# Swiglus in halves of 11 gate tiles instead of thirds, weight-block sums written over their blocks, and the last swiglu with all high parts before all low parts

## The chip, the cores and the metric

The kernel runs on one core of a Trainium2 chip. The metric is the device time of one execution in microseconds (us), and the time of a kernel is the median of its runs. Engines are named as in the profile: PE (TensorE matmul), PEld (its weight load), DVE (VectorE), ACT (ScalarE), POOL (GpSimd) and SP (SyncE, which here issues nearly all DMA).

## The reference

A two-layer diffusion transformer on 256 latent and 256 context tokens, width 1024, in float32. Each layer is swiglu, mixer, swiglu; layer 0 mixes with a short convolution, layer 1 with attention. Every step is modulated by vectors that come from matrix-vector products with `mod_w`.

```python
def _modulate(t, g, shift, scale):
    return _rms(t, g) * (1 + scale) + shift

def _swiglu(h, w13, w2):
    gte, up = jnp.split(h @ w13, 2, axis=-1)
    return (jax.nn.silu(gte) * up) @ w2
...
    for i in range(DEPTH):
...
        mod = (jax.nn.silu(c) @ mod_w[i] + mod_b[i]).reshape(bsz, 3, 3, 1, D_MODEL)
        modc = (jax.nn.silu(c_ctx) @ mod_w[i] + mod_b[i]).reshape(3, 3, D_MODEL)
        lat = lat + 0.5 * mod[:, 0, 2] * _swiglu(_modulate(lat, norm_g[i, 0], mod[:, 0, 0], mod[:, 0, 1]), ffn_w13[i, 0], ffn_w2[i, 0])
...
        lat = lat + mod[:, 1, 2] * y
...
        lat = lat + 0.5 * mod[:, 2, 2] * _swiglu(_modulate(lat, norm_g[i, 2], mod[:, 2, 0], mod[:, 2, 1]), ffn_w13[i, 1], ffn_w2[i, 1])
    return lat
```

The hidden width is 2816, which is 22 gate tiles of 128. The context tokens go through the first swiglu of layer 0, the convolution, the second swiglu of layer 0 and the first swiglu of layer 1; the last swiglu of layer 1 works on the 256 latent tokens alone.

## The kernel before

**Precision.** A float32 product is made of three fast matmuls: each operand is split into a high part (ACT copies it to the reduced format, L107) and a low part (DVE subtracts, L108), and `mm3` (L127) adds high×high, high×low and low×high in PSUM. So every weight costs ACT one pass and DVE one pass before PE may use it. Halves of split weights are tiles `wh`/`wl` of 1024 columns (4 of each, L110).

**Stages.** Opening; swiglu `ffn(0, 0)`; convolution mixer; its output product (`cw_out`); `ffn(0, 1)`; `ffn(1, 0)`; attention; the last swiglu. The residual `x` lies with features on partitions and 512 tokens (256 latent, 256 context) on columns.

**`ffn` (L632)** goes through the 22 gate tiles in three parts of 8, 7 and 7 (`THIRDS`). In each part it first makes the part's gate tiles g and then calls `project` (L483), which multiplies them with the part's rows of w2 for the 8 output tiles m and adds the result to `x` (L467: two instructions of 256 columns for each m and part). A raw tile of w2 holds two m's; each m is split in one piece of 1024 or 896 columns.

**`Pair` (L554)** computes one gate tile's two products (gate and up, 512 tokens each) with seven half-size products instead of eight. In a pair, `head` uses the blocks A11 and A12 of the weight, `five` the sum S1, `six` S2 and S4, `seven` S3, `four` A22; 84 matmuls of 256 columns in all. PE runs them as `head`, `five`, the previous pair's `seven`, `six`, the previous pair's `four`. `sums` (L572) makes S1 to S4 from the raw weight `wr` with three DVE instructions (L578 1024 columns; L584 and L588 512 columns) into a tile `ws` of its own, of which there is one; then ACT and DVE split `ws`. Three raw tiles `wr` are shared by all weight and modulation loads (`load_raw`, L101), which SP issues one after the other. The DVE ends of a pair are `sg` (L618, waits for `six`), `gm` (L629, waits for `four`) and the sum p (L623, waits for `seven`). All but 12 of the 66 gate tiles of these three swiglus go this way, 54 pairs; the others go as plain products (`w13_mm`, L540).

**Modulation.** 224 units (L151, one DVE instruction over 128x1024 each, four or two to a raw tile of 1 MB) make the modulation vectors. `tick(n)` (L190) issues n of them at fixed places in the program: `ev` after each output tile of a projection, 0.5 in each pair, 3 in a plain gate tile, 6 in each step of the convolution.

**Order.** A list scheduler sets the order of instructions on each engine from the program's order and its own estimates; every engine then runs its own list in order. Only the opening, parts of the attention and the start of the last swiglu are written out by hand.

**End of a projection.** Where a projection ends a stage, the last two m's are done in token halves so that the norm of the latent half starts early (`late`, L526). `square_add` (L231) sums the squares for the norm on DVE, 256 columns at a time.

**Last swiglu (L1567 on).** Activations hold high and low part side by side in 512 columns. `mm2` (L1432) issues for each block the high weight against 512 columns, then the low weight against the 256 high columns.

Of the kernel before, what the change touches and what calls it, by code (L numbers as in the profile page):

```python
# [16 lines left out]
P = 128  # L17
# [5 lines left out]
THIRDS = (8, 7, 7)  # L23

AS_IS = {(0, 0): range(3, 8), (0, 1): (), (1, 0): ()}
# [15 lines left out]
def hybrid_kernel(ctx: ExitStack, tc: tile.TileContext, a: dict, out: bass.AP):  # L41
# [5 lines left out]
    gp = ctx.enter_context(tc.tile_pool(name="gp", bufs=8))  # L47
# [47 lines left out]
    sccol = const.tile([P, KT, 32], F32, name="sccol", tag="sccol")  # L95
# [135 lines left out]
    def square_add(k, c0, c1):  # L231

        n = c1 - c0
        sq = tp.tile([P, T2], F32, name=nm("sq"), tag="gm", bufs=3)
        nc.scalar.activation(out=sq[:, :n], in_=x[:, k, c0:c1], func=AF.Square)
        for s in range(2):
            if c0 <= s * S < c1:
                part = sq[:, s * S - c0 : s * S - c0 + S]
                if k == 0:
                    accs[s] = tp.tile([P, S], F32, name=nm("acc"), tag=f"acc{s}", bufs=1)  # L240
                    nc.vector.tensor_copy(accs[s], part)
                elif k < KT - 1:
                    nc.vector.tensor_tensor(out=accs[s], in0=accs[s], in1=part, op=ALU.add)
                else:
                    accs[s, "last"] = part
# [237 lines left out]
    def project(ws, src, nk, gate, tail, tot, late, ev, between=()):  # L483
# [10 lines left out]
        nf = 3 if between else 2  # L494
        ahead = {}

        def get(m):
            for i in range(m, min(m + 3, KT)):
                if i not in ahead:
                    ahead[i] = ws(i)  # L500
            return ahead[m]

        w2 = [get(m) for m in range(nf)]
        p2 = [psum("py") for _ in range(nf)]
        cut = nk - 2 if between else nk - 1
        for i in range(nf):
            products(p2[i], w2[i], range(cut), 0, tot)
            if i < len(between):
                between[i]()
        if between:  # L510
            for i in range(nf):
                products(p2[i], w2[i], (nk - 2,), 0, tot)
        for i in range(nf):
# [4 lines left out]
        for m in range(nf, KT - late):  # L518
# [6 lines left out]
            tick(ev)  # L525
# [27 lines left out]

    class Pair:  # L554
# [11 lines left out]
        def keep(self, keys, part):  # L566
            hi, lo = half()
            split(hi, lo, part)
# [3 lines left out]
        def sums(self, n):  # L572

            a21, a22, a11, a12 = (self.raw[:, i * T2 : i * T2 + T2] for i in range(4))
            tt = nc.vector.tensor_tensor
            if n == 0:
                self.sm = sm = wp.tile([P, 2048], F32, name=nm("ws"), tag="ws", bufs=1)
                tt(  # L578
                    out=sm.rearrange("p (a b c) -> p a b c", a=2, b=2)[:, :, 0, :],
                    in0=a21.unsqueeze(1).to_broadcast([P, 2, T2]),  # L580
                    in1=self.raw[:, T2 : 3 * T2].rearrange("p (a c) -> p a c", a=2),
                    op=ALU.subtract,
                )
                tt(out=sm[:, T2:1024], in0=a11, in1=sm[:, :T2], op=ALU.subtract)  # L584
                self.keep(("S1", "S2"), sm[:, :1024])
                return
            sm = self.sm
            tt(out=sm[:, 3 * T2 :], in0=a12, in1=sm[:, T2:1024], op=ALU.subtract)  # L588
            self.keep(("S3", "S4"), sm[:, 1024:])
            self.w["A22"] = [  # L590
                wp.tile([P, T2], F32R, name=nm(t), tag=t, bufs=2) for t in ("w4h", "w4l")
            ]
            split(*self.w["A22"], a22)
# [38 lines left out]
    def ffn(l, b, h, tot, gate, tail, gs=(), ev=1.5):  # L632
        gs = list(gs)
        i0 = 0
        for t, n in enumerate(THIRDS):
            between = ()
            if tot == T2:
# [22 lines left out]
                for i in range(len(gs), n):  # L660
                    if t == 0 and not heads and i in AS_IS[l, b]:
# [15 lines left out]
                        else:  # L677
                            tick(3)
# [31 lines left out]
            box = {}  # L710

            def ws2(m):
                if m // 2 not in box:
                    src = a["w2a"][l, b, m // 2] if t == 0 else a["w2b"][l, b, t - 1, m // 2]
                    box[m // 2] = load_raw(src, 2 * n * P)
# [1011 lines left out]
```

## Time and profile before

| | |
|---|---|
| median of 3 runs | 1584.11 us (1583.46 to 1584.88) |
| the profiled execution's own time | 1585.98 us |
| its span, first to last instruction | 1584.1 us |
| mean granted TensorE clock | 0.991 |
| PE busy | 1562.8 us (99%) |
| DVE busy | 1318.2 us (83%) |
| ACT busy | 731.5 us (46%) |
| DMA | 248.74 MB, mean 157 GB/s |

PE's stages lie as follows (us of the span): opening to 55, `ffn(0, 0)` 55 to 378, convolution 378 to 519, `cw_out` 519 to 565, `ffn(0, 1)` 565 to 913, `ffn(1, 0)` 914 to 1270, attention 1271 to 1392, last swiglu 1392 to 1580. Matmuls are pipelined: what one costs PE is the distance between two starts, not the duration shown. The granted clock is 1.00 at full speed; a stretch of half speed costs half its length.

### The profile page before, as it was taken

How to read it: one execution, taken by the hardware profiler on the slowest of the kernel's cores; microseconds unless marked ns; L12 is line 12 of the kernel's file. 1: busy time of each engine (PE TensorE's matmuls, PEld its weight loads, DVE VectorE, ACT ScalarE, POOL GpSimd, SP SyncE). 2: the span in 40 equal slices, each digit the busy share in tenths (PEclk: the TensorE clock that was granted, in tenths of full speed). 3: DMA queues.
4: the chain of work that ended last, by engine and by line, in shares of the span. 5: the costliest groups of instructions: out<-in, count | busy, mean ns of one | idle time of the engine just before them, and what ended most of it. 6: DMA issues, size and time to landing. Idle time of an engine off the chain costs nothing.

```text
span 1584.1 us, 24975 instructions
## 1 busy us (share of the span) xinstructions
PE 1562.8 (99%) x10192; PEld 1425.7 (90%) x10192; DVE 1318.2 (83%) x2001; ACT 731.5 (46%) x1165; POOL 34.2 (2%) x28
## 2 busy tenths in 40 slices
PE   9999999999999999999999999999999989999998
PEld 7788998999878899989899899899889889998887
DVE  5788889879998879889799899898898886788654
ACT  4522552535222366335346375345245255765543
POOL 0000000000000000000000000000000002320000
PEclk8999999999999999999999999999999989999999
DMA  9355234334465422532443423543543652257552
GB/s 347 149 208 211 81 124 159 130 125 156 160 221 204 160 80 81 186 134 103 174 162 105 175 80 110 183 145 121 195 170 124 237 171 98 95 173 266 186 203 90
DMA packets 40771, 248.74 MB, mean 157 GB/s; under 512 B 5456, under 2 KB 8016, under 8 KB 15696
## 3 DMA queue, kind: packets, MB, share of 16 engines
q1 hardware_dynamic: 39936, 246.97, 44.2%
q8 instruction: 80, 1.31, 0.3%
q14 instruction: 35, 0.29, 0.1%
q10 hardware_dynamic: 720, 0.17, 0.0%
HBM read 244.77 MB, written 1.05 MB: 155 GB/s over the span
## 4 chain that ended last, share of the span: by engine, by line
PE 87%; DVE 6%; DMA 4%; ACT 1%; issue 1%; POOL 0%; ACTq 0%; DVEq 0%; SPq 0%; POOLq 0%
PE py L131 7%; PE py L132 7%; PE py L133 7%; PE p L133 6%; PE p L132 6%; PE p L131 6%; PE q L133 5%; PE q L131 5%; PE q L132 5%; DMA wr<-in_modT 3%; PE py L1433 3%; PE pu L1433 2%; PE pg L1433 2%; DVE junk L151 2%; DVE wl L108 1%; PE pg L131 1%
## 5 line engine op out<-in xcount | busy, mean ns | idle before, releaser
L107 ACT ACTIVATE wh<-wr 128x1024 fp32r<-128x1024 f32 (+2 forms) x258 | 263.4, 1032 | 337.7 <-PE py L132 96.1
L108 DVE TENSOR_TENSOR wl<-wr,wh 128x1024 fp32r<-128x1024 f32 (+2 forms) x258 | 304.6, 1188 | 64.6 <-ACT wh L107 62.2
L151 DVE CUSTOM_DVE_ANT_0 junk<-wr,scbc,modb 128x1024 bf16<-128x1024 f32 x224 | 286.6, 1280 | 31.4 <-DMA wr<-in_modT 29.0
L132 PE MATMUL py<-gl,wh 128*128 128x512 f32 (+1 forms) x570 | 213.3, 374 | 1.5 <-DVE gl L108 1.5
L131 PE MATMUL py<-gh,wh 128*128 128x512 f32 (+1 forms) x570 | 213.3, 374 | 0.0
L133 PE MATMUL py<-gh,wl 128*128 128x512 f32 (+1 forms) x570 | 213.0, 374 | 0.0
L108 DVE TENSOR_TENSOR wl<-ws,wh 128x1024 fp32r<-128x1024 f32 x108 | 130.2, 1221 | 24.6 <-ACT wh L107 24.4
L107 ACT ACTIVATE wh<-ws 128x1024 fp32r<-128x1024 f32 x108 | 113.1, 1057 | 66.6 <-PE p L132 32.2
L132 PEld LDWEIGHTS py<-gl,wh 128*128 128x128 f32 x570 | 107.4, 188 | 20.0 <-DVE gl L108 1.9
L133 PEld LDWEIGHTS py<-gh,wl 128*128 128x128 f32 x570 | 107.3, 188 | 19.1
L131 PEld LDWEIGHTS py<-gh,wh 128*128 128x128 f32 x570 | 107.4, 188 | 18.6
L133 PE MATMUL p<-th,wl 128*128 128x256 f32 x432 | 122.3, 283 | 0.0
L132 PE MATMUL p<-tl,wh 128*128 128x256 f32 x432 | 122.2, 283 | 0.0
L131 PE MATMUL p<-th,wh 128*128 128x256 f32 x432 | 122.2, 283 | 0.0
L131 PE MATMUL q<-bh,wh 128*128 128x256 f32 x320 | 90.9, 284 | 0.0
L133 PE MATMUL q<-bh,wl 128*128 128x256 f32 x320 | 90.8, 284 | 0.0
L132 PE MATMUL q<-bl,wh 128*128 128x256 f32 x320 | 90.8, 284 | 0.0
L131 PEld LDWEIGHTS p<-th,wh 128*128 128x128 f32 x432 | 82.9, 192 | 0.3
L132 PEld LDWEIGHTS p<-tl,wh 128*128 128x128 f32 x432 | 82.9, 192 | 0.3
L133 PEld LDWEIGHTS p<-th,wl 128*128 128x128 f32 x432 | 82.9, 192 | 0.0
L467 DVE SCALAR_TENSOR_TENSOR x<-py,G,x 128x256 f32<-128x256 f32 x144 | 62.3, 476 | 8.5 <-PE py L133 8.4
L578 DVE TENSOR_TENSOR ws<-wr 128x1024 f32<-128x1024 f32 x54 | 65.7, 1217 | 1.2 <-DMA wr<-in_w 1.1
(332 smaller groups left out, 4211.3 us busy)
## 6 DMA issues: line engine op xcount, KB each, us to landing
wr<-in_w SPq DMA_DIRECT2D x85, 1024.0 KB, 4.9
wr<-in_modT SPq DMA_DIRECT2D x64, 1024.0 KB, 4.9
wr<-in_w2b SPq DMA_DIRECT2D x24, 896.0 KB, 4.6
wr<-in_w2a SPq DMA_DIRECT2D x12, 1024.0 KB, 4.9
mr<-in_mod SPq DMA_DIRECT2D x16, 512.0 KB, 9.1
wr<-in_cw_cx SPq DMA_DIRECT2D x8, 1024.0 KB, 4.8
wr<-in_w2l SPq DMA_DIRECT2D x8, 1024.0 KB, 4.9
wr<-in_cw_b SPq DMA_DIRECT2D x4, 1024.0 KB, 5.0
```

The costliest lines, as they stand in the source:

```text
L107: nc.scalar.activation(out=hi, in_=src, func=AF.Copy)
L108: nc.vector.tensor_tensor(out=lo, in0=src, in1=hi.bitcast(F32), op=ALU.subtract)
L131: nc.tensor.matmul(ps, wh, mh, start=first, stop=False, **kw)
L132: nc.tensor.matmul(ps, wh, ml, start=False, stop=False, **kw)
L133: nc.tensor.matmul(ps, wl, mh, start=False, stop=last, **kw)
L151: nc.vector.tensor_tensor_reduce(out=junk, in0=raw[:, j * D : j * D + D], in1=scbc[:, v, :], scale=1.0, scalar=modb[:, l, col : col + 1], ...
L467: nc.vector.scalar_tensor_tensor(out=x[:, m, s * S : s * S + S], in0=ps[:, o : o + S], scalar=g[:, m, s : s + 1], in1=x[:, m, s * S : s * ...
L578: tt(out=sm.rearrange("p (a b c) -> p a b c", a=2, b=2)[:, :, 0, :], in0=a21.unsqueeze(1).to_broadcast([P, 2, T2]), in1=self.raw[:, T2 : 3 ...
L1433: nc.tensor.matmul(ps, w[0], m, start=first, stop=False, skip_group_check=True)
```

## The change

The matrix products stay the same in number and size. What changes:

1. **Halves.** `ffn` goes through the gate tiles in two parts of 11 (`NH`). So there are two projections in a swiglu instead of three, each with 11 gate tiles (33 matmuls of 512 columns for an m instead of 24 or 21), and `x` is updated 16 times instead of 24. w2 is loaded m by m (704 KB) and split in two pieces of 768 and 640 columns. The g tiles have 11 buffers. At the start of a projection two output tiles (before: three) are begun beside the last pair's `seven` and `four`.
2. **In place.** The tile `ws` is gone. The sums are written over the raw blocks: L592 over A22 and A21, L596 over A11, L599 over A12. The raw tile's blocks lie in another order in memory, and the split of A22 moves ahead of the sums.
3. **Modulation.** More of it is issued beside the output tiles (`ev` 1.5 to 3.3, 1.9 to 3.5, 2.1 to 3.2; `cw_out` 1.5 to 1.8), 4 instead of 3 in a plain gate tile, 5 instead of 6 in a convolution step, none after the last m ahead of the token halves. By stage the units go from 28 + 15 + 19 (gate tiles and projection of the three parts of `ffn(0, 0)`) to 43 + 33, in the convolution from 47 to 37, in `ffn(0, 1)` from 50 to 55, in `ffn(1, 0)` from 47 to 36, after it from 15 to 20.
4. **Norm sums.** One accumulator of 512 columns; its first square is written by ACT, without a copy on DVE.
5. **High parts first.** In the last swiglu and its projection `mm2` issues all high weights of a tile and then all low weights.

```diff
-THIRDS = (8, 7, 7)
-
-AS_IS = {(0, 0): range(3, 8), (0, 1): (), (1, 0): ()}
+NH = NM // 2
+
+PLAIN = {(0, 0): 8, (0, 1): 2, (1, 0): 2, (1, 1): NM}
...
         sq = tp.tile([P, T2], F32, name=nm("sq"), tag="gm", bufs=3)
         nc.scalar.activation(out=sq[:, :n], in_=x[:, k, c0:c1], func=AF.Square)
...
+        if k < KT - 1:
+            acc = accs["t"][:, c0:c1]
+            nc.vector.tensor_tensor(out=acc, in0=acc, in1=sq[:, :n], op=ALU.add)
+        else:
+            accs[c0 // S, "last"] = sq[:, :n]
...
+        nf = 2
         w2 = [get(m) for m in range(nf)]
         p2 = [psum("py") for _ in range(nf)]
-        cut = nk - 2 if between else nk - 1
-        for i in range(nf):
-            products(p2[i], w2[i], range(cut), 0, tot)
-            if i < len(between):
-                between[i]()
         if between:
+            products(p2[0], w2[0], range(nk // 2), 0, tot)
+            between[0]()
+            products(p2[0], w2[0], range(nk // 2, nk - 2), 0, tot)
+            between[1]()
+            products(p2[1], w2[1], range(nk - 2), 0, tot)
             for i in range(nf):
                 products(p2[i], w2[i], (nk - 2,), 0, tot)
...
-            tick(ev)
+            if not (tail and m == KT - late - 1):
+                tick(ev)
...
-            a21, a22, a11, a12 = (self.raw[:, i * T2 : i * T2 + T2] for i in range(4))
+            raw = self.raw
+            a22, a21, a11, a12 = (raw[:, i * T2 : i * T2 + T2] for i in range(4))
             tt = nc.vector.tensor_tensor
             if n == 0:
-                self.sm = sm = wp.tile([P, 2048], F32, name=nm("ws"), tag="ws", bufs=1)
+                self.w["A22"] = [
+                    wp.tile([P, T2], F32R, name=nm(t), tag=t, bufs=2) for t in ("w4h", "w4l")
+                ]
+                split(*self.w["A22"], a22)
                 tt(
...
+                    out=by_two(raw[:, :1024]), in0=a21.unsqueeze(1).to_broadcast([P, 2, T2]),
+                    in1=raw.rearrange("p (a b) -> p a b", a=2)[:, :, :T2], op=ALU.subtract,
                 )
-                tt(out=sm[:, T2:1024], in0=a11, in1=sm[:, :T2], op=ALU.subtract)
-                self.keep(("S1", "S2"), sm[:, :1024])
+                tt(out=a11, in0=a11, in1=a22, op=ALU.subtract)
+                self.keep(("S1", "S2"), raw.rearrange("p (a b) -> p a b", a=2)[:, :, :T2])
                 return
...
-            split(*self.w["A22"], a22)
+            tt(out=a12, in0=a12, in1=a11, op=ALU.subtract)
+            self.keep(("S3", "S4"), raw.rearrange("p (a b) -> p a b", a=2)[:, :, T2:])
...
-                            tick(3)
+                            tick(4)
...
+                        raws2[i] = load_raw(a["w2h"][l, b, t, i], n * P)
+                hs = []
+                for c0, c1 in ((0, 6 * P), (6 * P, n * P)):
+                    hi, lo = half()
+                    hs.append((hi, lo))
+                    split(hi[:, : c1 - c0], lo[:, : c1 - c0], raws2[m][:, c0:c1])
...
-    def mm2(ps, w, m, first, last):
-        nc.tensor.matmul(ps, w[0], m, start=first, stop=False, skip_group_check=True)
-        nc.tensor.matmul(
-            ps[:, :S], w[1], m[:, :S], start=False, stop=last, skip_group_check=True
-        )
+    def mm2(ps, w, m, nk):
+
+        for part in range(2):
+            n = S if part else T2
+            for k in range(nk):
+                for j, p in enumerate(ps):
+                    nc.tensor.matmul(
+                        p[:, :n], w(j, k)[part], m(k)[:, :n], start=not part and k == 0,
+                        stop=part == 1 and k == nk - 1, skip_group_check=True,
+                    )
```

**Where instructions move: the pairs.** DVE before, second part of `ffn(0, 0)`, while PE runs the pair whose gate is `sg_1470`; the sums `ws_1573` and the raw weight `wr_1567` belong to the next pair, `ws_1698` and `wr_1692` to the one after that:

```order
L108 TENSOR_TENSOR wl_1577<-ws_1573,wh_1576 128x1024
L108 TENSOR_TENSOR wl_1582<-ws_1573,wh_1581 128x1024
L618 TENSOR_TENSOR sg_1470<-q_1469,sg_1470 128x512
L578 TENSOR_TENSOR ws_1698<-wr_1692 128x2x512
L629 TENSOR_TENSOR gm_1417<-sg_1379,p_1377 128x512
L108 TENSOR_TENSOR w4l_1586<-wr_1567,w4h_1585 128x512
L584 TENSOR_TENSOR ws_1698<-wr_1692,ws_1698 128x512
L108 TENSOR_TENSOR gl_1551<-gm_1417,gh_1550 128x512
L588 TENSOR_TENSOR ws_1698<-wr_1692,ws_1698 128x512
L108 TENSOR_TENSOR wl_1695<-wr_1692,wh_1694 128x1024
L623 TENSOR_TENSOR p_1468<-p_1468,gm_1508 128x256
```

DVE in the changed kernel, the same stage; `sg_2344` is a pair's gate and `wr_2445` the raw weight of the next pair:

```order
L636 TENSOR_TENSOR gm_2262<-sg_2224,p_2222 128x512
L109 TENSOR_TENSOR wl_2448<-wr_2445,wh_2447 128x1024
L109 TENSOR_TENSOR gl_2429<-gm_2262,gh_2428 128x512
L109 TENSOR_TENSOR w4l_2452<-wr_2445,w4h_2451 128x512
L625 TENSOR_TENSOR sg_2344<-q_2343,sg_2344 128x512
L592 TENSOR_TENSOR wr_2445<-wr_2445 128x1024
L596 TENSOR_TENSOR wr_2445<-wr_2445 128x512
L599 TENSOR_TENSOR wr_2445<-wr_2445 128x512
L109 TENSOR_TENSOR wl_2458<-wr_2445,wh_2457 128x1024
L109 TENSOR_TENSOR wl_2463<-wr_2445,wh_2462 128x1024
L630 TENSOR_TENSOR p_2342<-p_2342,gm_2382 128x256
```

Before, the low parts of the next pair's sums (`wl_1577`, `wl_1582`) stand ahead of a pair's `sg`, and behind it the sums of the pair after next are made. Now the three sums of the next pair (L592, L596, L599) stand behind `sg` (L625), and their low parts (`wl_2458`, `wl_2463`) behind them.

PE in the changed kernel at the same place, the end of `seven` of the pair 2342 and the first products of S1 (into `q_2467`) and S2 (into `p_2466`); `wh_2457` and `wl_2458` are the split of L592's and L596's results:

```order
L133 MATMUL p_2342<-tl_729,wh_2338 128x256
L134 MATMUL p_2342<-th_728,wl_2339 128x256
L132 MATMUL q_2467<-th_724,wh_2457 128x256
L133 MATMUL q_2467<-tl_725,wh_2457 128x256
L132 MATMUL p_2466<-th_726,wh_2457 128x256
L133 MATMUL p_2466<-tl_727,wh_2457 128x256
L134 MATMUL q_2467<-th_724,wl_2458 128x256
L132 MATMUL q_2467<-th_724,wh_2457 128x256
```

Four products with the high parts of two sums stand ahead of the first product with a low part; in the program's order the twelve products of S1 come first, low part included.

**The turn from the first part to the next, in `ffn(1, 0)`.** DVE before, around the last `x` update of the first part (`py_10211`):

```order
L578 TENSOR_TENSOR ws_10250<-wr_10244 128x2x512
L467 TENSOR_SCALAR x<-py_10180,G_10036,x 128x256 x2
L584 TENSOR_TENSOR ws_10250<-wr_10244,ws_10250 128x512
L108 TENSOR_TENSOR w4l_10263<-wr_10244,w4h_10262 128x512
L588 TENSOR_TENSOR ws_10250<-wr_10244,ws_10250 128x512
L108 TENSOR_TENSOR w4l_10354<-wr_10335,w4h_10353 128x512
L108 TENSOR_TENSOR wl_10254<-ws_10250,wh_10253 128x1024
L108 TENSOR_TENSOR wl_10259<-ws_10250,wh_10258 128x1024
L467 TENSOR_SCALAR x<-py_10211,G_10036,x 128x256 x2
L108 TENSOR_TENSOR wl_10338<-wr_10335,wh_10337 128x1024
```

DVE in the changed kernel, around the last `x` update of the first half (`py_10729`):

```order
L152 ISA junk_10773,mod_5_10722<-wr_10771,scbc,modb 128x1024
L469 TENSOR_SCALAR x<-py_10729,G_10434,x 128x256 x2
L109 TENSOR_TENSOR wl_10778<-wr_10775,wh_10777 128x1024
L109 TENSOR_TENSOR w4l_10782<-wr_10775,w4h_10781 128x512
L592 TENSOR_TENSOR wr_10775<-wr_10775 128x1024
L109 TENSOR_TENSOR w4l_10872<-wr_10865,w4h_10871 128x512
L596 TENSOR_TENSOR wr_10775<-wr_10775 128x512
L592 TENSOR_TENSOR wr_10865<-wr_10865 128x1024
L599 TENSOR_TENSOR wr_10775<-wr_10775 128x512
L109 TENSOR_TENSOR wl_10788<-wr_10775,wh_10787 128x1024
L109 TENSOR_TENSOR wl_10793<-wr_10775,wh_10792 128x1024
```

Before, the sums and splits of the first pair of the next part stand ahead of the last `x` update; now they all stand behind it, with modulation units ahead of it.

**The end of `ffn(1, 0)`.** DVE before, ahead of and behind the last whole `x` updates (the norm begins with `RECIPROCAL`):

```order
L243 TENSOR_TENSOR acc_12324<-acc_12324,sq_12471 128x256
L243 TENSOR_TENSOR acc_12326<-acc_12326,sq_12471 128x256
L151 ISA junk_12479,mod_7_12358<-wr_12475,scbc,modb 128x1024
L467 TENSOR_SCALAR x<-py_12488,G_10036,x 128x256
L151 ISA junk_12484,mod_8_12481<-wr_12482,scbc,modb 128x1024
L243 TENSOR_TENSOR acc_12324<-acc_12324,sq_12511 128x256
L467 TENSOR_SCALAR x<-py_12514,G_10036,x 128x256
L467 TENSOR_SCALAR x<-py_12542,G_10036,x 128x256
L108 TENSOR_TENSOR wl_12646<-wr_12643,wh_12645 128x1024
```

DVE in the changed kernel, at the same place:

```order
L109 TENSOR_TENSOR wl_12419<-wr_12358,wh_12418 128x768
L109 TENSOR_TENSOR wl_12423<-wr_12358,wh_12422 128x640
L213 TENSOR_SCALAR A_13778<-mod_7_12237,normg 128x8
L152 ISA junk_12412,mod_8_12409<-wr_12410,scbc,modb 128x1024
L152 ISA junk_12414,mod_8_12409<-wr_12410,scbc,modb 128x1024
L469 TENSOR_SCALAR x<-py_12426,G_10434,x 128x256 x2
L109 TENSOR_TENSOR wl_12466<-wr_12416,wh_12465 128x768
L245 TENSOR_TENSOR acc_12209<-acc_12209,sq_12462 128x512
L109 TENSOR_TENSOR wl_12470<-wr_12416,wh_12469 128x640
L469 TENSOR_SCALAR x<-py_12475,G_10434,x 128x256
```

Before, modulation units stand between the `x` updates of the token halves; now the last of them stands ahead of the last whole tile's update (`py_12426`).

120 lines of the change are left out of this document (51 added, 69 removed).

## The prediction

> **What bounds the kernel.** I read the page's busy shares first, then windows over a stretch of pairs and over the stretches in which the chart of the span shows PE below nine tenths, then the waits of PE inside those, and last the timelines of the engines in a pair.
>
> ```profile
> PE 1562.8 (99%) x10192; PEld 1425.7 (90%) x10192; DVE 1318.2 (83%) x2001; ACT 731.5 (46%) x1165; POOL 34.2 (2%) x28
> ```
>
> PE is the bound. With windows (columns: stretch, length, then busy time and count of PE, PEld, DVE, ACT, POOL, granted clock, DMA share, GB/s):
>
> ```profile
> 697.00:764.00 67.00, 67.00 (x561) 67.00 (x560) 56.31 (x72) 37.01 (x59) 0.00 (x0) 1.00 0.32 108
> 419.00:440.00 21.00, 19.08 (x83) 15.15 (x82) 18.34 (x26) 4.26 (x6) 0.00 (x0) 1.00 0.56 201
> 560.00:575.00 15.00, 13.68 (x102) 13.25 (x101) 10.34 (x21) 9.21 (x20) 0.00 (x0) 0.89 0.15 46
> 886.00:892.00 6.00, 4.51 (x20) 3.38 (x19) 4.10 (x6) 2.28 (x3) 0.00 (x0) 1.00 0.44 157
> 1156.00:1163.00 7.00, 3.96 (x20) 3.33 (x19) 6.05 (x9) 2.89 (x4) 0.00 (x0) 0.81 0.38 146
> 1259.00:1290.00 31.00, 26.51 (x174) 24.82 (x173) 26.10 (x52) 13.98 (x25) 0.00 (x0) 0.83 0.57 196
> ```
>
> In the pairs (first row) PE has no idle time at all, so nothing can be gained there, only lost, and DVE is busy for 84%. What can be gained lies in the five other rows: 1.9, 1.3, 1.5, 3.0 and 4.5 us idle, and beside the second, fourth and fifth a lower clock, worth 15 x 0.11 = 1.7, 7 x 0.19 = 1.3 and 31 x 0.17 = 5.3 us. That the clock follows idle time is seen in these rows: the two waits of about 1.5 us left it at 1.00, those above 2.5 us did not. PE's waits in those stretches, in their order (the last three belong to the ten us behind the fourth stretch and, two of them, to the fifth), are
>
> ```profile
> PE pv L133 <- DVE wl L108: 1.9, 2, 1.4
> PE pg L131 <- ACT wh L107: 0.7, 1, 0.7
> PE py L132 <- DVE gl L108: 1.5, 1, 1.5
> PE p L131 <- ACT wh L107: 2.5, 1, 2.5
> PE ss L255 <- ACT sq L235: 2.1, 1, 2.1
> PE p L133 <- DVE wl L108: 0.5, 1, 0.5
> PE ss L269 <- DVE ri L264: 0.6, 1, 0.6
> PE pq L132 <- DVE hl L288: 0.9, 2, 0.7
> ```
>
> **The pairs.** The matmuls stay, one each 0.12 us from start to start (a pair: 84 x 0.12 = 10.08 us):
>
> ```profile
> 205.80 0.28 PE L132 MATMUL p<-tl,wh 128*128 128x256 f32 x1
> 205.92 0.28 PE L133 MATMUL p<-th,wl 128*128 128x256 f32 x1
> ```
>
> Before, DVE finishes the split of the next pair's sums ahead of `sg`, in the same 10 us in which it was asked for:
>
> ```profile
> 207.32 0.43 DVE L623 TENSOR_TENSOR p<-p,gm 128x256 f32<-128x256 f32 x1 [0.57 <-PE p L133]
> 207.66 1.28 DVE L151 CUSTOM_DVE_ANT_0 junk<-wr,scbc,modb 128x1024 bf16<-128x1024 f32 x1
> 208.86 2.36 DVE L108 TENSOR_TENSOR wl<-ws,wh 128x1024 fp32r<-128x1024 f32 x2
> 211.13 0.69 DVE L618 TENSOR_TENSOR sg<-q,sg 128x512 f32<-128x512 f32 x1
> 211.74 0.68 DVE L629 TENSOR_TENSOR gm<-sg,p 128x512 f32<-128x512 f32 x1
> 212.33 0.68 DVE L108 TENSOR_TENSOR w4l<-wr,w4h 128x512 fp32r<-128x512 f32 x1
> 212.93 1.22 DVE L578 TENSOR_TENSOR ws<-wr 128x1024 f32<-128x1024 f32 x1
> 214.07 0.68 DVE L108 TENSOR_TENSOR gl<-gm,gh 128x512 fp32r<-128x512 f32 x1
> ```
>
> From start to start that is 0.6 us for 512 columns and 1.14 for 1024. After the change the order on DVE puts the three sums of a pair behind `sg` of the pair before, which waits for PE's `six`, and the split behind the sums. The trace of before has one place in that manner, where only L584 and L588 stand behind `sg`:
>
> ```profile
> 1168.86 0.69 DVE L618 TENSOR_TENSOR sg<-q,sg 128x512 f32<-128x512 f32 x1 [0.66 <-PE q L133]
> 1169.47 0.68 DVE L584 TENSOR_TENSOR ws<-wr,ws 128x512 f32<-128x512 f32 x1
> 1170.19 2.01 ACT L107 ACTIVATE wh<-ws 128x1024 fp32r<-128x1024 f32 x2
> 1171.28 1.22 DVE L108 TENSOR_TENSOR wl<-ws,wh 128x1024 fp32r<-128x1024 f32 x1 [0.40 <-ACT wh L107]
> 1168.47 0.28 PE L133 MATMUL q<-bh,wl 128*128 128x256 f32 x1
> 1172.56 0.38 PE L133 MATMUL q<-th,wl 128*128 128x256 f32 x1
> ```
>
> From the start of `six`'s last matmul (1168.47) to the first product with S1's low part (1172.56) are 4.09 us, with 32 other matmuls between, which would take 33 x 0.12 = 3.96: PE was just caught. Two kinds of pairs alternate in the new order, and for each I go along this chain.
>
> *Kind one* (the pair shown in the order, `wr_2445`): all three sums stand behind `sg`. L592 comes into the chain: 4.09 + 1.14 = 5.23 us. PE has 36 matmuls to do first (20 of the head, 12 of `seven`, 4 with high parts), so it wants the low part at 37 x 0.12 = 4.44. Stall 0.79.
>
> *Kind two* (the pair ahead of it): DVE has `sg`, `gm`, the low part of A22, L592, `gl`, L596, and then ACT splits. `gm` waits for the 12 matmuls of `four` and starts at 1.44 + 0.39 = 1.83 (0.39 is `sg`'s distance from PE in the rows above); then 0.6 + 0.6 + 1.14 + 0.6 bring L596 to 4.77, its end to 5.46, ACT's high part (1.01 as one of the 2.01 above, and 0.1 for the two handovers) to 6.6. PE has 48 matmuls and wants the high part at 49 x 0.12 = 5.88. Stall 0.7. The low part follows behind the sum p (0.34 from start to start) and mostly a modulation unit (1.2), at about 9.0; PE, shifted by 0.7, wants it then too, so nothing is added.
>
> So 1.5 us for two pairs, 0.75 for one. Each of the six halves has a first pair that is priced below; for the other 48 that makes 36 us. Lower bound 0: the DVE list could run earlier than I trace it (DVE has 16% to spare and loses some 20 us of work in these stages, below). Upper bound 1.1 a pair, 53 us, if the modulation unit also delays kind two. I take 0.75, because the place at 1168 is the same chain short of one instruction. What is late next is `sg` itself: it waits for `six`, so the lead that DVE had is not won back in the next pair.
>
> [...]
>
> **The turn between the two halves.** Modulation units now fill DVE beside the last output tiles of the first half, and the second half's first sums come behind the last `x` update. In `ffn(1, 0)`, from the start of the last projection matmul: `x` at 0.39 (two, 0.39 each), low part of A11/A12 at 1.18, of A22 2.32, L592 2.92, another low part of A22 4.06, L596 4.66 to 5.35, ACT to 6.4, then L599 delays the low part to 7.0, ready 8.3. PE has the head (24) and four high parts: 0.23 + 28 x 0.12 = 3.6. Stall 4.7, and as it comes in pieces above 2.5 us, half clock as at 1156 for 1.7. By the same count `ffn(0, 1)` stalls 2.5 (two sums and two splits behind `x`) and `ffn(0, 0)` 0.7 (L596 alone). Together +9.6; bounds 3 and 14.
>
> **What goes.** The rows that carry it:
>
> ```profile
> 1150.75 7.06 DMA wr<-in_w
> 1254.18 7.83 DMA wr<-in_modT
> 1265.06 7.45 DMA wr<-in_wq
> L151 DVE CUSTOM_DVE_ANT_0 junk<-wr,scbc,modb 128x1024 bf16<-128x1024 f32 x224 | 286.6, 1280 | 31.4 <-DMA wr<-in_modT 29.0
> L467 DVE SCALAR_TENSOR_TENSOR x<-py,G,x 128x256 f32<-128x256 f32 x144 | 62.3, 476 | 8.5 <-PE py L133 8.4
> ```
>
> - 1156: the second turn between parts of `ffn(1, 0)`, where a weight waited 7.06 us behind modulation loads in SP's queue. With two parts it doesn't exist: -3.0 idle, -1.3 clock, and 1.1 of the following 10 us (0.5 of waiting for `wl` and the rest of the half clock): -5.4.
> - 1259 to 1290: the last modulation loads and units stand before and between the token halves; `wq` (7.45 us) is asked for behind them. Now none stands behind the last whole tile, SP asks for `wq` behind only one more load, and the first token half is covered by five gate tiles of products instead of three. Of 9.8 us I take 7.8; the norm's chain (`ri`, 0.6, and `hl`, 0.9 in the trace) stays, about 2. Bounds 3 and 9.8.
> - 419: ten modulation units fewer in the convolution, 12.8 us of DVE: -1.9 (bounds 0 and 1.9). 560: the second weight's high part is earlier on ACT: -1.8 of 3.0. 886: `gl` now has 9 x 3 x 0.228 = 6.2 us of projection behind `four` (0.228: below), before 15 x 0.228 = 3.4: -1.5.
> - DVE: 48 of the 144 updates of `x` fall away (48 x 0.476 = 22.8 us) and the copies of the square sums; w2's second split piece for each m gives a little back. All beside PE, so 0 by itself; where PE waits for DVE it is in the counts above. The loads of w2 move the same bytes in 16 instead of 12 issues on SP; the DMA share of 0.3 in pairs hides them.
>
> **High parts first.** A pair of matmuls of the last swiglu takes 0.353 us (three in 1.06 us), and the two alone 0.228 (five in 1.14 us) and 0.12:
>
> ```profile
> 1440.60 0.40 PE L1433 MATMUL pg<-h,wh 128*128 128x512 f32 x1
> 1441.66 0.40 PE L1433 MATMUL pu<-h,wh 128*128 128x512 f32 x1
> 879.67 0.39 PE L131 MATMUL py<-gh,wh 128*128 128x512 f32 x1
> 880.81 0.39 PE L133 MATMUL py<-gh,wl 128*128 128x512 f32 x1
> ```
>
> So 5 to 6 ns for each of 448 pairs, 2.7 us; I give back 1 for the low halves of w2, which are now wanted together and whose split DVE does last: -1.7 (bounds -2.7 and +2). The end, fold and output, stays.
>
> **Sum.** +36 +9.6 -5.4 -7.8 -1.9 -1.8 -1.5 -1.7 = +25.5 us, against the profiled execution 1585.98 + 25.5 = 1611.5. The runs' median stands 1.87 lower: 1609.6, say 1610.
>
> **Rivals.**
> - *Faster: the pairs stay hidden.* If DVE's and ACT's lists keep 0.8 us more lead than I count, all 36 us fall away: 1584.1 - 20.1 + 9.6 = 1574, and with cheap turns 1567. For it: high parts first on PE give cover at all places, and DVE's load falls. Against it: the place at 1168. The point that decides is 10.5 / 48 = 0.22 us a pair. Chance 0.28.
> - *Only one kind stalls.* About 18 us: 1592. For it: kind two has only the hand count behind it, kind one a row. Chance 0.23.
> - *The clock.* If each wait of 0.8 us costs 1.7 us of half clock, as the one at 1156 did, in half of the pairs: 24 x 1.7 = 41 more, 1651. Against it: 1.00 at 419 and 886. Chance 0.05.
> - The gains elsewhere just cancel: within 0.2% (3.2 us, about what a measurement of this kernel can tell from no change). Chance 0.03.
>
> **Numbers.** The likeliest, stalls in both kinds, has 0.41 and its own range 1598 to 1624. For 8 in 10 the range goes to most of the faster case, 1568, and leaves out the clock: 1626. Faster 0.28, same 0.03, slower 0.69.
>
> **What would show it.** Windows over pairs in which PE's busy time is 7% below the length; waits of PE q for `wl` or p/q for `wh`, 0.7 to 0.8 us each, one for each pair, in the chain of waits now DVE L592 and L596; three turns with 0.7, 2.5 and 4.7 us idle; no wait at the former 1156; a pair of last-swiglu matmuls at 0.347 us. Wrong it would be if a pair still takes 10.08 us: then DVE runs ahead of what the order lets one see. If pairs are slow but PE waits for a DMA, the raw tiles, held longer now by the sums, are the cause and not the order.

## The result and the profile after

| | before | changed |
|---|---|---|
| median | 1583.78 us (1582.18 to 1584.88, 4 runs) | 1637.57 us (1634.31 to 1639.38, 4 runs) |
| ratio | | 1.0338 (95% interval 1.0318 to 1.0358) |
| span of the profiled execution | 1584.1 us | 1637.6 us |
| granted clock | 0.991 | 0.990 |

The change makes the kernel 3.4% slower, 54 us. Slower had been forecast, but 1610 with a range up to 1626: twice the predicted loss came.

From the page of the changed kernel, the busy shares and two rows of its list of the costliest groups (behind the bar: busy time, mean ns, idle time before them and its releaser):

```profile
PE 1581.1 (97%) x10264; PEld 1435.7 (88%) x10264; DVE 1304.9 (80%) x1948; ACT 736.7 (45%) x1189; POOL 34.2 (2%) x28
L132 PE MATMUL q<-th,wh 128*128 128x256 f32 x216 | 66.8, 309 | 23.0 <-ACT wh L108 23.0
L134 PE MATMUL q<-th,wl 128*128 128x256 f32 x216 | 65.0, 301 | 11.5 <-DVE wl L109 11.5
```

PE's share falls from 99% to 97% and no other engine's share rises: none is busier, they wait for each other. `q<-th,wh` and `q<-th,wl` are the products with S1, high and low part. Windows over pairs, as in the prediction:

```profile
250.00:316.00 66.00, 62.56 (x506) 60.83 (x505) 56.60 (x74) 34.87 (x54) 0.00 (x0) 1.00 0.28 96
1165.00:1260.00 95.00, 89.73 (x724) 87.22 (x723) 82.26 (x105) 51.46 (x80) 0.00 (x0) 1.00 0.32 113
```

Before there was no idle PE time in pairs; now it is 5%, and 95 us hold 724 matmuls instead of 95 / 0.12 = 792. To see where all 54 us are, I sum, for each stretch, by how much the distance between the starts of two matmuls exceeds PE's own pace in the changed kernel (0.120 us for 256 columns, the mean of 79 starts from 238.20 to 247.67; 0.227 for 512, of 27 starts from 1135.12 to 1141.24). It counts idle time, half clock (0.50 granted, as from 218 to 220) and restarts alike:

| us above PE's own pace | before | changed | difference | forecast |
|---|---|---|---|---|
| pairs | 1.8 | 47.5 | +46 | +36 |
| turns between the parts of a swiglu | 5.3 | 14.9 | +10 | +9.6 -5.4 = +4 |
| end of `ffn(0, 0)`, convolution | 2.8 | 5.1 | +2 | -1.9 |
| around the norm behind `cw_out` | 3.3 | 1.9 | -1.4 | -1.8 |
| end of `ffn(0, 1)` | 3.0 | 3.0 | 0 | -1.5 |
| end of `ffn(1, 0)` to attention | 9.6 | 6.6 | -3 | -7.8 |
| attention | 3.4 | 3.7 | 0 | 0 |
| last swiglu | 2.7 | 1.9 | -0.7 | -1.7 |

The differences add up to 53. The rest is that PE has 72 matmuls more (10264 instead of 10192): the token halves of the longer projections run 72 products of 512 columns as 144 of 256, which costs 144 x 0.120 - 72 x 0.227 = 0.9 us.

**One period of two pairs** in the changed kernel. Kind one (all three sums behind `sg`), DVE and ACT and then PE:

```profile
244.22 0.69 DVE L625 TENSOR_TENSOR sg<-q,sg 128x512 f32<-128x512 f32 x1 [0.28 <-PE q L134]
244.83 1.22 DVE L592 TENSOR_TENSOR wr<-wr 128x1024 f32<-128x1024 f32 x1
246.08 0.69 DVE L596 TENSOR_TENSOR wr<-wr 128x512 f32<-128x512 f32 x1
246.81 2.96 ACT L108 ACTIVATE wh<-wr 128x1024 fp32r<-128x1024 f32 x3 [0.96 <-DVE wr L596]
247.90 2.36 DVE L109 TENSOR_TENSOR wl<-wr,wh 128x1024 fp32r<-128x1024 f32 x2 [0.40 <-ACT wh L108]
243.83 0.28 PE L134 MATMUL q<-hh,wl 128*128 128x256 f32 x1
247.92 0.38 PE L132 MATMUL q<-th,wh 128*128 128x256 f32 x1
248.38 0.28 PE L133 MATMUL p<-tl,wh 128*128 128x256 f32 x1
249.18 0.38 PE L134 MATMUL q<-th,wl 128*128 128x256 f32 x1 [0.52 <-DVE wl L109]
249.40 0.28 PE L132 MATMUL q<-th,wh 128*128 128x256 f32 x1
```

From `six`'s last matmul (243.83) to the first low part (249.18) are 5.35 us; 5.23 was forecast. Kind two, in the same manner:

```profile
231.35 0.69 DVE L625 TENSOR_TENSOR sg<-q,sg 128x512 f32<-128x512 f32 x1 [2.52 <-PE q L134]
232.72 0.69 DVE L636 TENSOR_TENSOR gm<-sg,p 128x512 f32<-128x512 f32 x1 [0.68 <-PE p L134]
235.79 0.69 DVE L596 TENSOR_TENSOR wr<-wr 128x512 f32<-128x512 f32 x1
236.72 0.28 PE L134 MATMUL p<-th,wl 128*128 128x256 f32 x1
237.62 0.39 PE L132 MATMUL q<-th,wh 128*128 128x256 f32 x1 [0.62 <-ACT wh L108]
```

Here L596 starts 4.44 us behind `sg` (forecast 4.77 - 0.39 = 4.38), and PE's gap from 236.72 is 0.90 instead of 0.12. What releases PE, ACT and DVE in these rows is another engine, never a DMA, so the raw tiles, held longer by the sums, are not the cause.

**The turn in `ffn(1, 0)`**, SP, ACT and DVE:

```profile
1119.88 11.87 SPq L104 DMA_DIRECT2D wr<-in_modT  x4
1134.08 3.97 SPq L104 DMA_DIRECT2D wr<-in_w  x2
1141.46 1.06 ACT L108 ACTIVATE wh<-wr 128x1024 fp32r<-128x1024 f32 x1 [14.23 <-DMA wr<-in_w]
1139.02 1.28 DVE L152 CUSTOM_DVE_ANT_0 junk<-wr,scbc,modb 128x1024 bf16<-128x1024 f32 x1 [1.32 <-DMA wr<-in_modT]
1141.67 0.88 DVE L469 SCALAR_TENSOR_TENSOR x<-py,G,x 128x256 f32<-128x256 f32 x2 [1.36 <-PE py L134]
1144.41 1.22 DVE L592 TENSOR_TENSOR wr<-wr 128x1024 f32<-128x1024 f32 x1
1146.15 0.68 DVE L596 TENSOR_TENSOR wr<-wr 128x512 f32<-128x512 f32 x1
```

The order had shown the sums behind the last `x` update. In the trace nothing of the next pair could have run ahead of it: ACT had been idle for 14 us for want of the raw weight, which SP asked for only at 1134, behind four modulation loads. DVE itself was free from 1140.3 to 1141.7.

### The profile page after: what moved, and what is told of

It reads as the page before. It is cut to its first block, busy times and chain, and to the rows that moved or that the text cites. A ratio compares the mean times of both kernels' runs of the same rounds, so it can differ in the third digit from the quotient of the medians.

```text
span 1637.6 us, 25074 instructions
## 1 busy us (share of the span) xinstructions
PE 1581.1 (97%) x10264; PEld 1435.7 (88%) x10264; DVE 1304.9 (80%) x1948; ACT 736.7 (45%) x1189; POOL 34.2 (2%) x28
## 3 DMA queue, kind: packets, MB, share of 16 engines
HBM read 244.77 MB, written 1.05 MB: 150 GB/s over the span
## 4 chain that ended last, share of the span: by engine, by line
PE 71%; DVE 19%; ACT 5%; DMA 2%; issue 2%; POOL 0%; DVEq 0%; ACTq 0%
PE py L132 6%; PE py L133 6%; PE py L134 6%; PE py L1451 4%; PE q L134 4%; PE q L132 4%; PE p L134 4%; PE p L132 4%; PE p L133 4%; ACT wh L108 4%; DVE wr L592 3%; PE q L133 3%; DVE wl L109 3%; PE pg L1451 3%; PE pu L1451 3%; DVE junk L152 3%
## 5 line engine op out<-in xcount | busy, mean ns | idle before, releaser
L108 ACT ACTIVATE wh<-wr 128x1024 fp32r<-128x1024 f32 (+3 forms) x390 | 370.8, 984 | 397.3 <-PE py L133 115.5
L109 DVE TENSOR_TENSOR wl<-wr,wh 128x1024 fp32r<-128x1024 f32 (+3 forms) x390 | 435.1, 1135 | 83.4 <-ACT wh L108 45.1
L134 PE MATMUL py<-gh,wl 128*128 128x512 f32 (+1 forms) x594 | 217.4, 366 | 0.5 <-DVE wl L109 0.5
L134 PEld LDWEIGHTS py<-gh,wl 128*128 128x128 f32 x594 | 112.0, 189 | 18.6 <-DVE wl L109 0.7
L132 PEld LDWEIGHTS py<-gh,wh 128*128 128x128 f32 x594 | 112.1, 189 | 18.2 <-ACT wh L108 0.6
L133 PEld LDWEIGHTS py<-gl,wh 128*128 128x128 f32 x594 | 112.1, 189 | 17.5
L132 PE MATMUL q<-th,wh 128*128 128x256 f32 x216 | 66.8, 309 | 23.0 <-ACT wh L108 23.0
L625 DVE TENSOR_TENSOR sg<-q,sg 128x512 f32<-128x512 f32 x54 | 37.3, 691 | 53.1 <-PE q L134 51.8
L134 PE MATMUL q<-th,wl 128*128 128x256 f32 x216 | 65.0, 301 | 11.5 <-DVE wl L109 11.5
L626 ACT ACTIVATE sg<-sg 128x512 f32<-128x512 f32 x54 | 34.1, 631 | 81.2 <-DVE sg L625 79.5
```

Source lines behind the costliest of these rows:

```text
L108: nc.scalar.activation(out=hi, in_=src, func=AF.Copy)
L109: nc.vector.tensor_tensor(out=lo, in0=src, in1=hi.bitcast(F32), op=ALU.subtract)
L132: nc.tensor.matmul(ps, wh, mh, start=first, stop=False, **kw)
L133: nc.tensor.matmul(ps, wh, ml, start=False, stop=False, **kw)
L134: nc.tensor.matmul(ps, wl, mh, start=False, stop=last, **kw)
L625: nc.vector.tensor_tensor(out=self.sg, in0=self.q, in1=self.sg, op=ALU.add)
```

## The experiments

Ratios are to the kernel before, which was timed again beside each group of runs (medians 1582.12, 1581.93 and 1583.88 us).

Theories. *A*: writing the sums over the raw blocks ties them to the split of A22 (L592 overwrites it), and with that to one of the two buffers `w4h`/`w4l`, which comes free only when `four` of two pairs earlier is done; A1 says that this buffer is what holds the sums, A2 that it is the four halves `wh`/`wl` (A11 must be split before its block is overwritten). *C*: the pairs are slow because of the halves, the modulation and the w2 splits around them.

### In place alone, in the kernel before

```diff
-                self.sm = sm = wp.tile([P, 2048], F32, name=nm("ws"), tag="ws", bufs=1)
...
+                split(*self.w["A22"], a22)
...
+                    out=by_two(raw[:, :1024]), in0=a21.unsqueeze(1).to_broadcast([P, 2, T2]),
...
+                tt(out=a11, in0=a11, in1=a22, op=ALU.subtract)
...
+            tt(out=a12, in0=a12, in1=a11, op=ALU.subtract)
```

> The kernel before with the sums written over the raw blocks and nothing else of the change (no tile ws; thirds, modulation and mm2 as before). Theory A (writing in place ties the sums to the split of A22 and puts them behind sg): every pair loses 0.8 to 1.0 us as in the changed kernel, so 1584 + 43 to 54, 1627 to 1638 us, with waits of q for wh and wl in nearly every pair. Theory C (the pairs are slow because of the halves, the modulation beside them and the w2 splits): 1584 plus or minus 5 us and no such waits.

Measured: 1624.93 us, ratio 1.0264 (1.0244 to 1.0284). PE's waits:

```profile
PE q L131 <- ACT wh L107: 17.9, 26, 1.6
PE q L133 <- DVE wl L108: 9.8, 18, 1.0
```

PE, writing `q`, waits for ACT's high part and DVE's low part of S1: the same waits in thirds, with the old modulation and the old w2 splits, and 43 of the 54 us. C falls. The time is 2 us below the lower end that A gave, but so was the kernel before in this group. The pairs lose about 43 us above PE's pace (48.7 in their stretches, some 5.5 of it the old stall at the second turn of `ffn(1, 0)`).

### One more buffer for A22's split

Against the run in place:

```diff
-                    wp.tile([P, T2], F32R, name=nm(t), tag=t, bufs=2) for t in ("w4h", "w4l")
+                    wp.tile([P, T2], F32R, name=nm(t), tag=t, bufs=3) for t in ("w4h", "w4l")
```

> As the run in place, with three buffers instead of two for the split of A22 (w4h, w4l). Theory A1 (what holds the sums is the buffer of A22's split, which comes free only when four of two pairs earlier is done): the waits in the pairs go, below 0.2 us a pair, and the time is within 10 us of the kernel before, 1579 to 1594. Theory A2 (the four halves wh/wl hold them, because S1 is written over A11 and A11 must have been split): no change against the run in place, 1627 to 1638.

Measured: 1584.75 us, ratio 1.0021 (1.0005 to 1.0037). Windows over pairs, then DVE and, last, PE in one of them (L590 and L593 are L596 and L599 of the changed kernel, L619 is `sg`):

```profile
165.00:226.00 61.00, 61.00 (x511) 61.00 (x510) 51.54 (x65) 33.93 (x53) 0.00 (x0) 1.00 0.29 102
696.00:757.00 61.00, 61.00 (x511) 61.00 (x510) 54.49 (x69) 34.78 (x54) 0.00 (x0) 1.00 0.33 114
206.93 0.69 DVE L590 TENSOR_TENSOR wr<-wr 128x512 f32<-128x512 f32 x1
209.80 1.22 DVE L108 TENSOR_TENSOR wl<-wr,wh 128x1024 fp32r<-128x1024 f32 x1
210.94 0.68 DVE L619 TENSOR_TENSOR sg<-q,sg 128x512 f32<-128x512 f32 x1
214.82 0.28 PE L133 MATMUL q<-th,wl 128*128 128x256 f32 x1
```

The pairs are whole again, with the sums still written in place: the sums and their low part stand ahead of `sg`, and PE takes the low part 3.8 us after DVE has it. A1 holds. The tie can be seen in the changed kernel, at the end of a `four`:

```profile
239.39 0.28 PE L133 MATMUL p<-tl,w4h 128*128 128x256 f32 x1
239.71 0.63 ACT L108 ACTIVATE w4h<-wr 128x512 fp32r<-128x512 f32 x1 [0.25 <-PE p L133]
```

ACT splits a new A22 as soon as `four` has read the high part of an old one for the last time. With two buffers this is the A22 of the next pair; with three, of the pair after next, and the sums have a pair's time more.

### One more half of each kind instead

Against the run in place:

```diff
-            wp.tile([P, 1024], F32R, name=nm(t), tag=t, bufs=4) for t in ("wh", "wl")
+            wp.tile([P, 1024], F32R, name=nm(t), tag=t, bufs=5) for t in ("wh", "wl")
```

> As the run in place, with five instead of four halves wh and wl, and two buffers for A22's split. Theory A1: no cure, 1622 to 1638 us, the waits stay above 0.7 us a pair. Theory A2: the waits go, 1579 to 1594 us.

Measured: 1612.38 us, ratio 1.0189 (1.0162 to 1.0217): 12.5 us better than in place alone, which neither theory gave. PE's waits:

```profile
PE q L131 <- ACT wh L107: 15.9, 24, 1.0
PE q L133 <- DVE wl L108: 8.8, 17, 0.5
```

The waits stay (41 instead of 44 of them), so A2 falls as the cause of the pairs. Of the gain, about 6 us are the old stall at the second turn of `ffn(1, 0)`, which is absent in this run; where the rest comes from stays open.

### The changed kernel with three buffers

```diff
-                    wp.tile([P, T2], F32R, name=nm(t), tag=t, bufs=2) for t in ("w4h", "w4l")
+                    wp.tile([P, T2], F32R, name=nm(t), tag=t, bufs=3) for t in ("w4h", "w4l")
...
-        t = tp.tile([P, S], F32, name=nm("t"), tag="t", bufs=3)
+        t = tp.tile([P, S], F32, name=nm("t"), tag="t", bufs=2)
...
+    cs2 = tp.tile([P, T2], F32, name="cs2", tag="acc", bufs=1)
+    cosT, sinT = cs2[:, :S], cs2[:, S:]
...
```

> The changed kernel with three buffers for A22's split (room made by two instead of three buffers of the norm's tiles t and by putting the two rotation tables into the accumulator's place). Theory A1: the 47 us of the pairs go and nothing else, or with it up to 10 of the 15 us at the turns between the halves: 1580 to 1592 us. Theory A2: 1635 to 1640 us. Theory C: above 1620 us.

Measured: 1595.24 us, ratio to the kernel before 1.0072 (1.0048 to 1.0096); 42 us better than the changed kernel, 3 us above the range. A window over pairs and PE's costliest waits:

```profile
1125.00:1220.00 95.00, 95.00 (x794) 95.00 (x793) 87.68 (x113) 53.45 (x83) 0.00 (x0) 1.00 0.40 134
PE q L132 <- ACT wh L108: 9.4, 5, 2.8
```

794 matmuls in 95 us: the pairs cost nothing any more. The turns didn't get cheaper but dearer (4.3, 6.4 and 8.1 us above PE's pace, 19 together, 15 in the changed kernel). So the turns have another cause than the pairs. The 42 us are not the third buffer's alone: two buffers for `t` take away a wait of 3.2 us by themselves (last experiment).

### Less modulation ahead of a turn

T1: the turns are slow because modulation loads stand ahead of the next half's first weight on SP's queue (and their units on DVE). T2: because of the sums in place.

```diff
-            if not (tail and m == KT - late - 1):
+            if m < KT - late - 1 if tail else m < 5:
                 tick(ev)
...
-                        tick(0.5, prev.seven())
+                        tick(1.0, prev.seven())
```

> The changed kernel, but no modulation units after output tiles 5, 6 and 7 of a first half; one unit instead of half of one in each pair takes their place. Theory T1 (the 15 us lost at the three turns between halves come from the modulation loads and units that stand ahead of the next half's first weight, on SP's queue and on DVE): 10 to 14 us of it go, 1637 - 12 = 1622 to 1628 us, the pairs staying as slow as they are. Theory T2 (the turns are slow because of the sums in place, like the pairs): 1634 us or more, or slower still by the added units in the pairs.

> Both repairs in the changed kernel: three buffers for A22's split and no modulation units after output tiles 5 to 7 of a first half. By T1 1595 - 12 to 18 = 1577 to 1583 us, about as fast as the kernel before or a little faster; by T2 1592 us or more.

Measured, in the changed kernel: 1619.96 us, ratio 1.0239 (1.021 to 1.0267). That is 17.6 us better than the changed kernel by the medians, 16 by the ratios (1.0338 - 1.0239), and 2 us below what T1 gave; some 4 us of it come from the pairs, the rest from the turns. With three buffers as well: 1580.62 us, ratio 0.9989 (0.9973 to 1.0004), not to be told from the kernel before. The turn in `ffn(1, 0)` without the third buffer:

```profile
1110.00:1145.00 35.00, 35.00 (x218) 31.67 (x217) 22.55 (x29) 12.69 (x18) 0.00 (x0) 1.00 0.33 119
1108.77 29.16 SPq L104 DMA_DIRECT2D wr<-in_w  x4
1118.31 1.22 DVE L592 TENSOR_TENSOR wr<-wr 128x1024 f32<-128x1024 f32 x1
1129.57 0.88 DVE L469 SCALAR_TENSOR_TENSOR x<-py,G,x 128x256 f32<-128x256 f32 x2 [1.07 <-PE py L134]
```

No idle time over the turn at 1129: T1 holds. SP asks for the weight 21 us ahead of the last `x` update, and the first pair's sums stand ahead of that update again. The sums in place do no harm there once the weight is early. The edit takes away loads and units together; how much each of the two costs was not measured.

### The same rule in the kernel before

```diff
-            tick(ev)
+            if m < KT - late - 1 if tail else m < 6:
+                tick(ev)
...
-                        tick(0.5, prev.seven())
+                        tick(1.0, prev.seven())
...
-        tick(6)
+        tick(5)
...
```

With `mm2` as in the change, and 4 units in a plain tile.

> The kernel before (thirds, sums in their own tile ws), with the modulation placed by the same rule: none after output tiles 6 and 7 of a part that is not the last, none after the last tile ahead of the token halves, one unit in each pair, 5 in a convolution step, 4 in a plain gate tile; and high parts first. If the losses at 1156 and 1259 come from modulation loads ahead of weights, they go, with those at 419: 1583 - 8 to 16 = 1567 to 1575 us. If they only move elsewhere: 1580 to 1586 us.

> The thirds with the modulation placed anew, and one output tile more without modulation units at the end of each stage (none after tile 4). If the 9 us still lost at the end of the third swiglu come from units and loads beside its last tiles: 4 to 8 us less, 1570 to 1574 us. If they come from the norm's own chain and wq: no change, 1576 to 1580 us.

Measured: 1577.68 us, ratio 0.9971 (0.9959 to 0.9983); and with one more tile free of units at the ends (`KT - late - 2`), 1577.24 us, ratio 0.9949 (0.9929 to 0.9968), the fastest here. The gain of 0.3% and 0.5% includes the high parts first. Both medians lie 3 us above what was expected. The stall at 1156 is gone in both. At the end of `ffn(1, 0)` 9.1 us above PE's pace remained in the first and 1.9 in the second, so that loss does come from units and loads beside the last tiles; but in attention, where the units put off now stand, 4.2 became 7.8, in waits for POOL's and DVE's part of the softmax. That the units on DVE delay that part would fit; it wasn't tried by itself.

> The halves with both repairs, and one output tile more without modulation units at the end of each stage. The loss left there is small (3.5 us at the end of the third swiglu), so 0 to 3 us less: 1577 to 1581 us; more only if units pushed into the last stage get in its way.

Measured, the same step in the halves: 1587.04 us, ratio 1.0025 (1.0013 to 1.0038), 6 us above the range and slower than without the step (0.9989). It is the case named at the end of what was expected. Here the units put off cost attention its output weights: SP issues `wo` behind three modulation loads, and PE waits for its split:

```profile
1358.54 10.72 SPq L104 DMA_DIRECT2D wr<-in_modT  x3
1370.13 3.52 SPq L104 DMA_DIRECT2D wr<-in_wo  x2
1380.76 0.58 PE L132 MATMUL py<-a,wh 128*128 128x256 f32 x1 [5.72 <-ACT wh L108]
```

### High parts first, alone

```diff
+        for part in range(2):
+            n = S if part else T2
+            for k in range(nk):
+                for j, p in enumerate(ps):
...
```

> The kernel before with all high parts ahead of all low parts in the last swiglu and its projection, alone. If the order costs 5 to 6 ns at each change of width: the stage from the first to the last matmul of those tiles is 2 to 3 us shorter. If the low parts of w2 come late: one or two waits of PE for wl of 0.4 us or more, and less than 2 us gained.

Measured in a single run: the tiles from gate tile 5 on take 118.26 us instead of 119.72, the projection 61.88 instead of 62.08 to its last matmul. That is 1.7 us, less than the 2 to 3 expected for this cost, and without the waits for `wl` that were to explain less. The 272 pairs of the gate tiles gave 5 ns each, the 176 of the projection 1 ns; why, stays open. In the changed kernel one wait of 0.6 us in that stage takes part of it. The run's whole time, 1580.89 us, lies within the spread of the kernel before.

### Two buffers for the norm's tiles

```diff
-        t = tp.tile([P, S], F32, name=nm("t"), tag="t", bufs=3)
+        t = tp.tile([P, S], F32, name=nm("t"), tag="t", bufs=2)
...
```

> The changed kernel with two instead of three buffers for the norm's tiles t, nothing else. Theory N (at the end of the first swiglu the last x update stands behind twelve norm instructions on DVE, and PE's norm sum waits 3.2 us for its square): with two buffers it stands behind fewer, the wait of 3.2 us falls below 1.5 us, and 2 to 4 us are gained. If the wait comes from the projection being longer or from the modulation units: it stays at 3 us.

Measured in a single run: 1633.54 us. Windows over the end of `ffn(0, 0)` in the changed kernel and, second, in this run:

```profile
380.00:410.00 30.00, 26.61 (x211) 26.44 (x210) 24.39 (x48) 13.16 (x25) 0.00 (x0) 0.94 0.41 156
```

```profile
380.00:410.00 30.00, 28.64 (x235) 27.89 (x234) 25.80 (x52) 12.18 (x24) 0.00 (x0) 1.00 0.40 141
```

2 us less idle time, and the clock stays whole: the wait of 3.2 us for the square of the last `x` is gone. Three buffers had let the scheduler put twelve norm instructions ahead of that `x` update.

## Why the prediction was wrong

The way was right, and so was the chain in the pairs. But 54 us came instead of 25.5, because three terms of the sum were too good: the pairs by 10 us, the turns by 6, the ends of the stages by 10.

**The pairs (+36, measured +46).** The mechanism is the one that was forecast, and so are its times: `sg` to the first low part, the place of L596 in kind two. PE's lateness is 0.81 us in kind one and 0.78 in kind two, 0.79 and 0.7 forecast. The term was mis-sized in two ways. Each of the three stops of the period (a short one at the first high part of kind one, 247.92, among them) cost PE more than the lateness: the two matmuls behind it start 0.22 us apart (as at 249.18 and 249.40), not 0.12, which makes 0.3 us. A period takes 22.03 us (236.72 to 258.75), not 20.16: 1.87 lost, where 1.5 was forecast, and over 48 pairs that makes 9 us. And the prediction left six first pairs to the turns, of which only three stand at a turn; the other three make some 3 us. In place, L596 starts 1.25 us behind L592 (244.83 to 246.08), which writes its operand, where 1.14 was counted. The lower bound of 0 and the rival "the pairs stay hidden" fall, and so does "only one kind".

**What holds the sums.** The prediction named the order on DVE; it didn't name the buffer that forces it. It spoke of the split of A22 only as an instruction in the chain. The third buffer shows that A22's split was the tie: with it the sums go back ahead of `sg`, and 40 us return where nothing else was changed.

**The turns (+9.6 and -5.4, measured +10 together).** The new cost was some 15 us instead of 9.6: about 4, 5 and 6 us at the three turns, where 0.7, 2.5 and 6.4 were forecast. The third came as counted: PE takes the first low part of S1 8.5 us behind the start of the last projection matmul, 8.3 forecast. At the other two, two steps failed. The count lets the last `x` update start 0.39 us behind the last projection matmul; in the trace DVE was still busy with sums at the first and with a modulation unit at the second, and `x` came 2.0 and 1.5 us behind:

```profile
211.12 0.39 PE L134 MATMUL py<-gh,wl 128*128 128x512 f32 x1
210.82 2.35 DVE L592 TENSOR_TENSOR wr<-wr 128x1024 f32<-128x1024 f32 x2
213.09 0.87 DVE L469 SCALAR_TENSOR_TENSOR x<-py,G,x 128x256 f32<-128x256 f32 x2
767.29 0.39 PE L134 MATMUL py<-gh,wl 128*128 128x512 f32 x1
767.59 1.28 DVE L152 CUSTOM_DVE_ANT_0 junk<-wr,scbc,modb 128x1024 bf16<-128x1024 f32 x1
768.79 0.87 DVE L469 SCALAR_TENSOR_TENSOR x<-py,G,x 128x256 f32<-128x256 f32 x2
```

And half clock was priced at the third turn alone, but it stands behind all three (windows as before):

```profile
216.80:220.80 4.00, 3.78 (x19) 3.78 (x20) 3.83 (x5) 1.18 (x2) 0.00 (x0) 0.59 0.42 113
774.40:778.40 4.00, 3.69 (x21) 3.69 (x22) 3.97 (x5) 1.52 (x3) 0.00 (x0) 0.64 0.22 37
1149.40:1153.40 4.00, 3.64 (x19) 3.64 (x20) 3.89 (x5) 1.65 (x3) 0.00 (x0) 0.58 0.38 90
```

At a granted clock of 0.50 the matmuls of 256 columns start 0.213 us apart instead of 0.120 (14 starts from 217.67 to 220.65; the same behind 1156 in the kernel before). So these stretches cost 44% of their length, not the half that was counted, and by the starts 1.2 to 1.5 us at each turn.

Behind this is the cause that the prediction didn't see: the raw weight is late at every turn (ACT idles 9.1, 12.1 and 14.2 us for it). The profile of before had the row for it, `wr<-in_w` 7.06 us behind modulation loads at 1150, and I used it only for the stall that goes. Putting more units beside the last tiles made the same stall at all three turns, and without them it is gone. What was counted as removed at 1156 was moved.

**The ends of the stages (-11.2, measured about -1).** The 1.9 at 419 came: PE's waits for `wl` in the convolution fall from 1.9 to 0.2 us. But a new wait of 3.2 us, with half clock behind it (0.50 from 402 to 404), stands at the end of `ffn(0, 0)`: an `x` update behind norm instructions, which I had not looked for because the change has no line for that order. `ffn(1, 0)` gave 3 of 7.8, since a wait of 1.5 us for a square and 0.9 for w2 splits at its last tiles came in place of the old ones. The 1.5 at 886 went too, and a wait of 0.8 us for a square at 956, with a clock of 0.57 from 958 to 962, came in its place.

**High parts first (-1.7).** The number was met alone (1.7) by luck: it was 2.7 less 1 for waits that didn't come, and the projection gave 0.2 of its share of 1. In the changed kernel it was 0.7.

**The clock.** The rival that the waits in the pairs would halve it falls: 1.00 in the windows over pairs above (66 and 95 us) and in those from 805 to 871 and 1016 to 1082, with waits of 0.5 to 0.7 us about every 10 us. In one place in the pairs it did fall, to 0.50 from 699 to 702, behind waits of 1.05 and 0.52 us; behind waits of 1.04 and 0.52 us at 883 and 885 it stayed at 1.00. But the prediction's reading that waits of 1.5 us leave the clock whole and only those above 2.5 us lower it is too simple. Its own rows have 0.89 at 560, where no wait is above 0.7 us, and behind the first turn, whose longest wait is 1.4 us, the clock is 0.59.

The range ended at 1626, which left room for one of these terms to be dearer; all three were.

## What to carry to other kernels

Writing the sums over their source saved a tile here and added waits (1624.93 us in place alone, against 1582.12): the sums became bound to the last reader of the block, and through it to the buffer that this reader fills. When a buffer is given up, look at which other ring of buffers now paces the producer; one more slot of it, 4 KB for each partition, was worth 40 us. And bulk loads that can go anywhere should not stand ahead of the next stage's first weight on the queue that they share: SP here asked for that weight at 1134.08, behind four modulation loads from 1119.88 on, and ACT idled 14.2 us for it. Put them where that weight has already been asked for, and check what the last of them delays.

## What the runs showed that was not expected

- The three stops of one period cost PE 0.1 us each beyond their own length: 0.22 instead of 0.12 us to the second matmul (237.62 to 237.84, 247.92 to 248.14 and 249.18 to 249.40). If that held at all 52 stops of q for `wh` and `wl` that the list of waits names, it would be 5 us, an estimate.
- One buffer more or less changes the scheduler's order far away: two buffers for a tile of the norm took away a wait of 3.2 us, and in the version with three buffers for A22's split the turns were 4 us dearer.
- The clock stayed at 1.00 in the windows over pairs, through waits of 0.5 to 0.7 us about every 10 us, and its mean over 4 us was 0.58 to 0.64 behind each of the three turns, whose longest waits were 1.4, 2.8 and 1.6 us. What length or sum of waits lowers it, these runs don't tell.
